# Attention: where the copies of V's last three pieces and of K's second half stand in the order

## The chip, the cores and the metric

The kernel runs on one core of one Trainium2 chip. The metric is the device time of one execution in microseconds (us). A profiled execution also gives a span, from the first instruction to the last, with the instructions of each engine in it: TensorE (PE, with its weight loads as PEld), VectorE (DVE), ScalarE (ACT), GpSimd (POOL) and SyncE (SP).

## The reference

One block of a streaming encoder on x (1 x 512 x 1024, float32) and a memory mem (1 x 256 x 1024): two recurrent branches side by side, merged into x; then attention from x into the memory; then a gated feed-forward layer with a short convolution; a final norm. The change lies in the attention:

```
def cross_attention(h, m, w_q, w_kv, w_o):
    q = (h @ w_q).reshape(bsz, s, X_HEADS, X_HEAD_DIM)          # 4 heads of 256
    kv = m @ w_kv
    k = kv[..., :D_MODEL].reshape(bsz, -1, X_HEADS, X_HEAD_DIM)
    v = kv[..., D_MODEL:].reshape(bsz, -1, X_HEADS, X_HEAD_DIM)
    sc = jnp.einsum('bqhd,bkhd->bhqk', q, k).astype(jnp.float32) * (X_HEAD_DIM ** -0.5)
    pr = jax.nn.softmax(sc, axis=-1).astype(v.dtype)
    o = jnp.einsum('bhqk,bkhd->bqhd', pr, v).reshape(bsz, s, D_MODEL)
    return o @ w_o
```

h is the normed x, m the normed memory.

## The kernel before

**Precision and tiles.** A float32 matrix product is done as three matmuls on a split operand: `hi` is the value rounded to the matmul's format, `lo` the rest. So each operand is first copied (ScalarE writes `hi`) and then subtracted (VectorE writes `lo`); `mm3` (lines 169 to 173) issues hi x hi, hi x lo and lo x hi. Weights come in pieces of 128 x 1024 through `stream` (lines 106 to 127): SyncE loads a piece (four buffers), ScalarE and VectorE split it (three buffers). `dense` (lines 192 to 200) makes one output block of 128 x 512 from one such piece, in 24 matmuls.

**What the stage is given.** K and V are computed from the memory at the start of the kernel and put away in DRAM (`dK`, `dV`), 1024 x 256 values each. The stage before attention is the merge into x (`mix_ps`); behind attention come its output product (`co_ps`) and the feed-forward layer.

**The attention stage** (lines 1057 to 1152). K and V are brought back in eight pieces of 128 x 512 by `load_kv`: four of K (`load_kv("K", 0)` for heads 0 and 1, `load_kv("K", 1)` for heads 2 and 3) and four of V (two rows of memory blocks, each in two halves, of which the first half serves heads 0 and 1). Every piece is loaded into one of five buffers (`KVB = 5`) by a load that ScalarE issues, then copied by ScalarE and subtracted by VectorE into K2 or V2 (lines 1094 and 1095). A piece's buffer comes free with its subtraction; pieces six to eight wait for the buffers of pieces one to three.

`q_head` makes a head's q in two blocks of 24 matmuls (`q_ps`) and splits it (lines 1107 and 1108). `attend` takes a head through: for each of four tiles of 128 queries, 6 matmuls of scores (`sc_ps`, two PSUM buffers), the maximum and a bias on VectorE (lines 1123 and 1124), exp on ScalarE (`ex`, line 1126), division by the sum, and two transposes on TensorE (`prT_ps`); then the split of the transposed probabilities (`prT`, lines 1133 and 1134), and two blocks of 6 matmuls with V (`o_ps`, one PSUM buffer), each split into `o2` (lines 1141 and 1142). The program is written as q of head 0, then for each head its attention and q of the next head; the second half of K is loaded and copied, in the text, behind q of head 1.

**What sets the order.** The text is not the order in which an engine works. A planner takes the instructions with their dependencies and lays out one sequence for each engine by its own estimate of when each could go, with the place in the text as priority, so that q of the next head is put among the scores of this one. On the chip each engine follows its sequence: an instruction that waits holds all that stands behind it on that engine, and a load that ScalarE issues has its place in ScalarE's sequence. `tc.issue_after(ins)` sets, for the planner, that what is written inside it comes behind `ins` on the same engine; it makes no signal. GpSimd in the meantime adds up feed-forward weights in DRAM (`dS`), each step held back to a matmul of this stage (`sum_behind`, lines 177 to 181); SyncE loads the weights ahead.

Of the kernel before, what the change touches and what calls it, by code (L numbers as in the profile page):

```python
# [3 lines left out]

# [54 lines left out]
def hybrid_block_kernel(ctx: ExitStack, tc: tile.TileContext, xT_d, mT_d, pv_d, cst_d, win_d, wk_d, wv_d,  # L59
                        lup_d, gup_d, rga_d, rgx_d, wba_d, wbb_d, wmix_d, wq_d, wo_d, wfi_d, wfo_d, out_d):  # L60
    nc = tc.nc
    V, S, PE = nc.vector, nc.scalar, nc.tensor
# [12 lines left out]
    def mm_ps(name):  # L75
        return pmm.tile([P, T], F32, tag="mm", name=name)

    def rw_ps(name, pool=None, tag="rw", **kw):
        return (pool or prw).tile([P, T], F32, tag=tag, name=name, **kw)
# [89 lines left out]
    def mm3(ps, lh, ll, rh, rl, start, stop, **kw):  # L169
        first = PE.matmul(ps, lh, rh, start=start, stop=False, **kw)  # L170
        PE.matmul(ps, lh, rl, start=False, stop=False, **kw)  # L171
        PE.matmul(ps, ll, rh, start=False, stop=stop, **kw)  # L172
        return first
# [18 lines left out]
    def dense(ps, units, rhs, nkb, nsum=0):  # L192

        for kb in range(nkb):
            wh, wl = units.next()
            rh, rl = rhs(kb)
            ins = mm3(ps, wh, wl, rh, rl, kb == 0, kb == nkb - 1)
            if kb * nsum % nkb < nsum:
                sum_behind(ins)
        return ins  # L200
# [845 lines left out]
    for m in range(KB):  # L1046
        xin = pm.tile([P, T], F32, tag="xin", name=f"xin{m}")
        nc.scalar.dma_start(xin, xT_d[:, m, :])
        ps = mm_ps(f"mix_ps{m}")
# [14 lines left out]
    def probs(hd):  # L1064
        return pk.tile([P, 2, 2, T], F32R, tag="prT", name=f"prT{hd}", bufs=2)
# [14 lines left out]
    V2 = pk.tile([P, 2, 2, D], F32R, name="V2")  # L1080

    def load_kv(what, i):
        for h in range(2):
            kv = pk.tile([P, T], F32, tag="kv", name=f"kv{what}{i}_{h}", bufs=KVB)
            if what == "K":
                ks = slice(4 * i + 2 * h, 4 * i + 2 * h + 2)
                hi, lo = K2[:, 0, ks], K2[:, 1, ks]
                kv = kv.rearrange("p (m n) -> p m n", n=NMEM)
                nc.scalar.dma_start(kv, dK[ks].rearrange("m p n -> p m n"))
            else:  # L1090
                cs = slice(h * T, (h + 1) * T)
                hi, lo = V2[:, 0, i, cs], V2[:, 1, i, cs]
                nc.scalar.dma_start(kv, dV[i, :, cs])
            S.copy(hi, kv)
            V.tensor_tensor(lo, kv, hi.bitcast(F32), ALU.subtract)

    load_kv("K", 0)
    for i in range(2):
        load_kv("V", i)
    uq = Units(wq_d, "wq")  # L1100

    def q_head(hd, nsum=2):
        q2 = pk.tile([P, 2, 2, T], F32R, tag="q2", name=f"q2_{hd}", bufs=2)
        for i in range(2):
            ps = mm_ps(f"q_ps{hd}_{i}")
            dense(ps, uq, lambda kb: (hx[:, 0, kb, :], hx[:, 1, kb, :]), KB, nsum + i * (nsum > 0))
            S.copy(q2[:, 0, i, :], ps)
            V.tensor_tensor(q2[:, 1, i, :], ps, q2[:, 0, i, :].bitcast(F32), ALU.subtract)
        return q2

    def attend(hd, q2):
        prT = probs(hd) if hd else prT0
        prps = [rw_ps(f"prT_ps{hd}_{i}", pat, "prT", bufs=2) for i in range(2)]
        for tt in range(4):
            sl = slice(tt * P, (tt + 1) * P)
            ps = rw_ps(f"sc_ps{hd}_{tt}", pat, "sc", bufs=2)
            for i in range(2):
                kb = 2 * hd + i
                PE.matmul(ps[:, :NMEM], q2[:, 0, i, sl], K2[:, 0, kb, :], start=(i == 0), stop=False)
                PE.matmul(ps[:, :NMEM], q2[:, 0, i, sl], K2[:, 1, kb, :], start=False, stop=False)  # L1120
                PE.matmul(ps[:, :NMEM], q2[:, 1, i, sl], K2[:, 0, kb, :], start=False, stop=(i == 1))
            st = pk.tile([P, 4], F32, tag="smst", name=f"smst{hd}_{tt}", bufs=4)
            V.tensor_reduce(st[:, 0:1], ps[:, :NMEM], AX.X, ALU.max)
            V.tensor_tensor(st[:, 1:2], st[:, 0:1], nrx[:, tt:tt + 1], ALU.mult)
            ex = pk.tile([P, NMEM], F32, tag="ex", name=f"ex{hd}_{tt}", bufs=3)
            S.activation(ex, ps[:, :NMEM], AF.Exp, scale=rxc[:, tt:tt + 1], bias=st[:, 1:2],
                         accum_out=st[:, 2:3])
            V.reciprocal(st[:, 3:4], st[:, 2:3])
            V.tensor_scalar(ex, ex, st[:, 3:4], None, ALU.mult)
            for i in range(2):  # L1130
                PE.transpose(prps[i][:, sl], ex[:, i * P:(i + 1) * P], ident)
        for i in range(2):
            S.copy(prT[:, 0, i, :], prps[i])
            V.tensor_tensor(prT[:, 1, i, :], prps[i], prT[:, 0, i, :].bitcast(F32), ALU.subtract)
        for i in range(2):
            kb = 2 * hd + i
            ps = rw_ps(f"o_ps{kb}", pat, "o")
            for n in range(2):
                cs = slice(kb * P, (kb + 1) * P)
                mm3(ps, V2[:, 0, n, cs], V2[:, 1, n, cs], prT[:, 0, n, :], prT[:, 1, n, :], n == 0, n == 1)  # L1140
            S.copy(o2[:, 0, kb, :], ps)
            V.tensor_tensor(o2[:, 1, kb, :], ps, o2[:, 0, kb, :].bitcast(F32), ALU.subtract)

    q2 = q_head(0, 0)
    for hd in range(4):
        attend(hd, q2)
        if hd < 3:
            q2 = q_head(hd + 1)
        if hd == 0:
            load_kv("K", 1)  # L1150

    pk_ctx.close()

# [25 lines left out]
    for m in order:  # L1179
        ps = mm_ps(f"co_ps{m}")  # L1180
# [4 lines left out]
        i = m % 4  # L1185
# [264 lines left out]
    for k in K4:  # L1450
        ks = slice(k, min(k + 4, HB))
# [11 lines left out]
    for k in K4:  # L1463
        ks = slice(k, min(k + 4, HB))
# [82 lines left out]
```

## Time and profile before

| | us |
|---|---|
| three runs | 885.95, 889.65, 891.37; median 889.65 |
| the profiled execution | 888.2 |
| its span | 886.4 |
| TensorE busy in it | 865.9 |
| VectorE, ScalarE, GpSimd busy | 676.7, 513.6, 132.5 |

The three runs lie within 0.6% of each other. Times in the trace are counted from the start of the span. "L1094" is line 1094 of the kernel before; `kvK<-dK` is an instruction that writes a buffer `kvK` from `dK`, with the numbers of the buffers left out. A busy TensorE is not TensorE at its peak: matmuls overlap, and their ends are modelled, so an idle stretch is read from what the profile lists as idle before an instruction.

### The profile page before, as it was taken

To read this page: it belongs to the slowest core of one execution; us is meant where nothing else is said; L and a number is where in the kernel's file an instruction comes from. 1 tells how busy PE (TensorE), PEld (TensorE's weight loads), DVE (VectorE), ACT (ScalarE), POOL (GpSimd) and SP (SyncE) were. 2 spreads that over 40 slices of the span, in tenths; PEclk is the share of its full clock that TensorE was granted. 3 is DMA by queue.
4 is the path that set the end of the run, shared out by engine and by line. 5 is a ranking of instruction groups with operands and counts; after the bars stand their busy time and mean duration, and the time that the engine had idled before them with its cause. 6 is when DMAs were issued, how large, how long until landed. Compare 5 with 4: busy or idle time off the path is not lost.

```text
span 886.4 us, 15940 instructions
## 1 busy us (share of the span) xinstructions
PE 865.9 (98%) x6197; PEld 755.0 (85%) x6197; DVE 676.7 (76%) x1096; ACT 513.6 (58%) x788; POOL 132.5 (15%) x163
## 2 busy tenths in 40 slices
PE   8999999999999999999989999999999999999996
PEld 7778878888877677888867778999999999999896
DVE  6796598777967777685565568898888788998674
ACT  7575676643337676243454456766665566767563
POOL 0101222021101012001112211112111211111100
PEclk9999999999999999999999999999999999999999
DMA  8878899678997379858877868899999999998963
GB/s 279 301 254 215 209 223 238 191 197 240 260 236 156 74 197 230 229 157 239 220 205 169 203 150 191 239 258 285 300 257 297 262 320 277 249 280 207 293 208 95
DMA packets 97562, 201.37 MB, mean 227 GB/s; under 512 B 19600, under 2 KB 30992, under 8 KB 97424
## 3 DMA queue, kind: packets, MB, share of 16 engines
q1 hardware_dynamic: 62240, 118.57, 40.5%
q0 software_dynamic: 25504, 67.38, 37.3%
q10 hardware_dynamic: 9744, 14.42, 4.9%
q8 instruction: 48, 0.79, 0.4%
q14 instruction: 26, 0.21, 0.1%
HBM read 188.54 MB, written 78.12 MB: 301 GB/s over the span
## 4 chain that ended last, share of the span: by engine, by line
PE 80%; DMA 8%; DVE 7%; ACT 3%; issue 1%; ACTq 0%; SPq 0%; DVEq 0%
PE in_ps L171 7%; PE in_ps L172 7%; PE in_ps L170 7%; PE fx_ps L170 3%; PE fx_ps L172 3%; PE fx_ps L171 3%; PE fyz_ps L170 3%; PE fyz_ps L171 3%; PE fyz_ps L172 3%; DMA wfi_r<-in_wfi 2%; DMA wfo_r<-dOs 2%; PE co_ps L172 2%; PE mix_ps L171 2%; PE co_ps L171 2%; PE mix_ps L170 2%; PE co_ps L170 2%
## 5 line engine op out<-in xcount | busy, mean ns | idle before, releaser
L171 PE MATMUL in_ps<-hT,win_h 128*128 128x512 f32 x304 | 121.0, 398 | 0.4 <-DVE hT L387 0.4
L172 PE MATMUL in_ps<-hT,win_l 128*128 128x512 f32 x304 | 121.3, 399 | 0.0
L170 PE MATMUL in_ps<-hT,win_h 128*128 128x512 f32 x304 | 120.5, 398 | 0.3 <-DVE pr L589 0.3
L136 ACT CAST wfi_h<-wfi_r 128x1024 fp32r<-128x1024 f32 x77 | 80.9, 1051 | 64.4 <-PE fyz_ps L171 17.2
L137 DVE TENSOR_TENSOR wfi_l<-wfi_r,wfi_h 128x1024 fp32r<-128x1024 f32 x77 | 93.9, 1220 | 23.5 <-ACT wfi_h L136 23.4
L485 POOL DMA_DIRECT2D dS<-in_wfi x66 | 66.7, 1034 | 299.2 <-PE in_ps L170 96.4
L171 PEld LDWEIGHTS in_ps<-hT,win_h 128*128 128x128 f32 x304 | 57.1, 188 | 14.6 <-DVE hT L387 1.0
L170 PEld LDWEIGHTS in_ps<-hT,win_h 128*128 128x128 f32 x304 | 57.1, 188 | 13.4 <-DVE pr L589 0.7
L172 PEld LDWEIGHTS in_ps<-hT,win_l 128*128 128x128 f32 x304 | 57.1, 188 | 12.9 <-issue 0.7
L521 POOL DMA_DIRECT2D dOs<-in_wfo x54 | 39.8, 784 | 171.3 <-PE fx_ps L170 46.0
L123 DVE TENSOR_TENSOR win_l<-win_r,win_h 128x1024 fp32r<-128x1024 f32 x38 | 46.3, 1220 | 24.1 <-ACT win_h L122 20.6
L122 ACT CAST win_h<-win_r 128x1024 fp32r<-128x1024 f32 x38 | 39.9, 1050 | 40.0 <-PE in_ps L171 35.6
L1358 DVE TENSOR_TENSOR wfo_l<-wfo_r,wfo_h 128x1024 fp32r<-128x1024 f32 (+1 forms) x39 | 46.9, 1206 | 14.4 <-ACT wfo_h L1357 14.4
L1357 ACT CAST wfo_h<-wfo_r 128x1024 fp32r<-128x1024 f32 (+1 forms) x39 | 40.3, 1035 | 30.3 <-DMA wfo_r<-dOs 14.0
L172 PE MATMUL ox_ps<-go,wfo_l 128*128 128x256 f32 x176 | 48.8, 277 | 1.2 <-DVE wfo_l L1358 1.2
L170 PE MATMUL ox_ps<-go,wfo_h 128*128 128x256 f32 x176 | 48.7, 277 | 0.6 <-ACT wfo_h L1357 0.6
L170 PE MATMUL fx_ps<-hr,wfi_h 128*128 128x256 f32 x176 | 48.7, 277 | 0.3 <-ACT sn L1293 0.3
L170 PE MATMUL fx_ps<-hq,wfi_h 128*128 128x256 f32 x176 | 48.8, 277 | 0.1
L172 PE MATMUL fyz_ps<-hq,wfi_l 128*128 128x256 f32 x176 | 48.7, 277 | 0.0
L172 PE MATMUL fx_ps<-hq,wfi_l 128*128 128x256 f32 x176 | 48.7, 277 | 0.0
L170 PE MATMUL fyz_ps<-hq,wfi_h 128*128 128x256 f32 x176 | 48.7, 277 | 0.0
L171 PE MATMUL fx_ps<-hq,wfi_h 128*128 128x256 f32 x176 | 48.6, 276 | 0.0
(432 smaller groups left out, 2689.7 us busy)
## 6 DMA issues: line engine op xcount, KB each, us to landing
dS<-in_wfi POOLq DMA_DIRECT2D x66, 512.0 KB, 7.6
wfi_r<-dS SPq DMA_DIRECT2D x44, 512.0 KB, 6.9
win_r<-in_win SPq DMA_DIRECT2D x38, 512.0 KB, 5.3
wfi_r<-in_wfi SPq DMA_DIRECT2D x33, 512.0 KB, 5.6
dS<-dS POOLq DMA_DIRECT2D x22, 512.0 KB, 5.7
dOs<-in_wfo POOLq DMA_DIRECT2D x12, 512.0 KB, 7.8
wk_r<-in_wk SPq DMA_DIRECT2D x8, 512.0 KB, 5.8
wv_r<-in_wv SPq DMA_DIRECT2D x8, 512.0 KB, 5.2
```

The source lines that it names most:

```text
L122: casts.append(S.copy(hi[:, o:o + n], raw[:, o:o + n]))
L123: V.tensor_tensor(lo[:, o:o + n], raw[:, o:o + n], hi[:, o:o + n].bitcast(F32), ALU.subtract)
L136: S.copy(hi, raw)
L137: V.tensor_tensor(lo, raw, hi.bitcast(F32), ALU.subtract)
L170: first = PE.matmul(ps, lh, rh, start=start, stop=False, **kw)
L171: PE.matmul(ps, lh, rl, start=False, stop=False, **kw)
L172: PE.matmul(ps, ll, rh, start=False, stop=stop, **kw)
L485: return lambda: nc.gpsimd.dma_start(s(out), src, **kw)
L521: yield lambda k=k, w=w, src=src: nc.gpsimd.dma_start(dO[n, m][:, k * P:(k + w) * P], src, **kw)
L1357: S.copy(hi[:, :n], raw[:, :n])
L1358: V.tensor_tensor(lo[:, :n], raw[:, :n], hi[:, :n].bitcast(F32), ALU.subtract)
```

## The change

`load_kv` now only issues the two loads and returns what is to be split; the new `split_kv` makes the copies and subtractions, and can put the copies, on ScalarE, behind a given instruction. The first half of K and the first piece of V are loaded and split as before. The other three pieces of V are loaded at the same place in the text, but their copies are written behind q of head 0 and ordered behind the copy of q's second block (`last["q"]`). The second half of K is loaded, in the text, ahead of head 0's attention, and its copies are written ahead of q of head 1 and ordered behind the second copy of head 0's transposed probabilities (`last["p"]`). The number of loads, copies, subtractions and matmuls, and the buffers and their order, stay as they were.

```
     def load_kv(what, i):
+        copies = []
         for h in range(2):
             kv = pk.tile([P, T], F32, tag="kv", name=f"kv{what}{i}_{h}", bufs=KVB)
...
                 nc.scalar.dma_start(kv, dV[i, :, cs])
-            S.copy(hi, kv)
+            copies.append((hi, lo, kv))
+        return copies
+
+    def split_kv(copies, behind=None):
+        for hi, lo, kv in copies:
+            with tc.issue_after(behind.ins) if behind is not None else nullcontext():
+                S.copy(hi, kv)
             V.tensor_tensor(lo, kv, hi.bitcast(F32), ALU.subtract)
 
-    load_kv("K", 0)
-    for i in range(2):
-        load_kv("V", i)
+    split_kv(load_kv("K", 0))
+    vs = load_kv("V", 0)
+    split_kv(vs[:1])
+    vs = vs[1:] + load_kv("V", 1)
     uq = Units(wq_d, "wq")
...
-            S.copy(q2[:, 0, i, :], ps)
+            last["q"] = S.copy(q2[:, 0, i, :], ps)
...
-            S.copy(prT[:, 0, i, :], prps[i])
+            last["p"] = S.copy(prT[:, 0, i, :], prps[i])
...
+    last = {}
     q2 = q_head(0, 0)
+    split_kv(vs, last["q"])
+    ks = load_kv("K", 1)
     for hd in range(4):
         attend(hd, q2)
+        if hd == 0:
+            split_kv(ks, last["p"])
         if hd < 3:
             q2 = q_head(hd + 1)
-        if hd == 0:
-            load_kv("K", 1)
```

More of the change, by code (lines that the diff above doesn't have):

```diff
@@ L1 @@
 import math
-from contextlib import ExitStack
+from contextlib import ExitStack, nullcontext
 from itertools import chain, islice
```

## The prediction

> **What bounds the kernel now.** I read the page first, then the busy time by stretch, then the chain of waits inside the attention stage, then the instructions of ScalarE, TensorE and VectorE around the one hole that the stretches show.
>
> ```profile
> span 886.4 us, 15940 instructions
> ...
> PE 865.9 (98%) x6197; PEld 755.0 (85%) x6197; DVE 676.7 (76%) x1096; ACT 513.6 (58%) x788; POOL 132.5 (15%) x163
> ```
>
> TensorE is busy 865.9 of 886.4 us, so everything that any change without touching its matmuls can win in the whole kernel is 20.5 us, and only what is lost in the stage that is edited is in reach here. The next view gives stretches: length, busy time of TensorE (and how many matmuls), its weight loads, VectorE, ScalarE, GpSimd, then the granted clock, the DMA share and GB/s.
>
> ```profile
> 430.00:450.34 20.34, 20.34 (x93) 16.36 (x91) 12.74 (x22) 11.31 (x18) 1.87 (x2) 1.00 0.85 222
> 450.34:458.50 8.16, 4.48 (x26) 3.63 (x25) 3.54 (x10) 2.29 (x7) 1.87 (x2) 1.00 0.78 246
> 458.50:521.00 62.50, 62.50 (x320) 49.43 (x321) 35.78 (x89) 27.30 (x59) 13.05 (x14) 1.00 0.79 175
> 521.00:560.00 39.00, 39.00 (x187) 32.41 (x186) 32.59 (x63) 26.49 (x51) 6.73 (x7) 1.00 0.76 177
> 560.00:800.00 240.00, 239.48 (x2096) 238.23 (x2096) 213.91 (x287) 157.21 (x227) 39.70 (x55) 1.00 0.95 277
> ```
>
> The attention stage lies in the first three rows. TensorE is full in the first and the third; in 450.34 to 458.50 it loses 8.16 - 4.48 = 3.68 us. That is all the stage has to give. The clock is 1.00 throughout, so the hole costs its own length and nothing behind it. The chain of waits says what the hole is:
>
> ```profile
> 445.44 4.27 DMA kvV<-dV
> 449.75 7.43 DMA kvK<-dK
> 457.20 0.62 ACT K L1094
> ```
>
> A load of K's second half, issued at 449.75, lands 7.43 us later; the copy of it (0.62 us) is on the path. ScalarE's own order shows why (ACTq rows are loads that it issues; the bracket is idle time before the row and what ended it):
>
> ```profile
> 444.51 0.62 ACT L1094 CAST V<-kvV 128x512 fp32r<-128x512 f32 x1
> 444.52 1.31 ACTq L1093 DMA_DIRECT2D kvV<-dV  x3
> 446.95 1.05 ACT L122 CAST wq_h<-wq_r 128x1024 fp32r<-128x1024 f32 x1 [1.82 <-PE q_ps L171]
> 448.41 1.95 ACT L1094 CAST V<-kvV 128x512 fp32r<-128x512 f32 x3 [0.41 <-DMA kvV<-dV]
> 449.75 0.90 ACTq L1089 DMA_DIRECT2D kvK<-dK  x2
> 450.27 1.06 ACT L1107 CAST q<-q_ps 128x512 fp32r<-128x512 f32 x2
> 457.20 0.62 ACT L1094 CAST K<-kvK 128x512 fp32r<-128x512 f32 x1 [5.87 <-DMA kvK<-dK]
> 457.73 0.56 ACT L1126 ACTIVATE ex<-sc_ps,smst,rxn 128x256 f32<-128x256 f32 x1
> ...
> 464.36 1.07 ACT L1133 CAST prT<-prT_ps 128x512 fp32r<-128x512 f32 x2 [1.26 <-PE prT_ps L1131]
> 467.18 0.59 ACT L1141 CAST o<-o_ps 128x512 fp32r<-128x512 f32 x1 [1.74 <-PE o_ps L172]
> ```
>
> The first exp of head 0 (457.73) stands behind a copy of K that head 2 alone reads, and that copy sits 5.87 us on its load. On VectorE the bias of that exp (L1124, two of them in 0.28 us) was there long before:
>
> ```profile
> 454.29 0.28 DVE L1124 TENSOR_TENSOR smst<-smst,rxn 128x1 f32<-128x1 f32 x2
> 457.85 0.69 DVE L1095 TENSOR_TENSOR K<-kvK,K 128x512 fp32r<-128x512 f32 x1 [3.29 <-ACT K L1094]
> ...
> 467.80 0.69 DVE L1142 TENSOR_TENSOR o<-o_ps,o 128x512 fp32r<-128x512 f32 x1 [1.53 <-ACT o L1141]
> ```
>
> So the exp was ready at 454.29 + 0.14 = 454.43 and ran at 457.73, 3.30 us late. TensorE's rows show what that did:
>
> ```profile
> 441.49 0.39 PE L170 MATMUL q_ps<-hx,wq_h 128*128 128x512 f32 x1
> ...
> 446.98 0.39 PE L170 MATMUL q_ps<-hx,wq_h 128*128 128x512 f32 x1
> ...
> 450.90 0.39 PE L1119 MATMUL sc_ps<-K,q 128*128 128x256 f32 x1 [0.55 <-ACT q L1107]
> ...
> 458.43 0.38 PE L1119 MATMUL sc_ps<-K,q 128*128 128x256 f32 x1 [3.14 <-ACT ex L1126]
> ...
> 465.00 0.50 PE L170 MATMUL o_ps<-prT,V 128*128 128x512 f32 x1
> ...
> 486.99 0.28 PE L1119 MATMUL sc_ps<-K,q 128*128 128x256 f32 x1
> ```
>
> Two holes, 0.55 + 3.14 = 3.69 us, the 3.68 of the stretch. The second: the third score tile needs one of two PSUM buffers, which the late exp holds. The first: the scores wait for q's copy. A block of 24 q matmuls takes 446.98 - 441.49 = 5.49 us, 0.229 each; head 0's second block ended by 447.2, but its q was copied at 450.27, behind three copies of V.
>
> **K's second half behind the probabilities.** Same two loads, two copies and two subtractions; nothing is added, and an order on one engine needs no new signal. The copies leave their place ahead of the first exp and go behind the prT copies, which end at 464.36 + 1.07 = 465.43. Then the exp goes at 454.43, frees its score buffer at about 455.0, and TensorE, which had q matmuls to 455.1 (458.43 less 3.14, less the overlap of the last one), does not wait: the 3.14 us go whole. Next late would be the second exp, 0.56 us behind the first, as before. At the new place the copies need 2 x 0.62 = 1.24 us of ScalarE, in a gap of 1.74 ahead of the o copy, and 2 x 0.69 = 1.38 us of VectorE in a gap of 1.53: cost 0. Were the gaps gone, at most 1.4 us would come ahead of the o copy, and head 1's q matmuls stand beside it. The reader of these pieces, head 2's scores at 486.99, is 20 us off.
>
> The loads move too: written ahead of head 0's attention, they can be issued right behind V's three, from 444.52 + 1.31 = 445.83, for 0.90 us, before the weight copy at 446.95. What is queued behind them on ScalarE is that copy and q's; the second load also needs the buffer of V's first piece (copied by 444.51 + 0.62 = 445.13, then the 0.69 us subtraction: 445.8), so it adds at most some tenths. Landing 7.43 us after 446.7 they are there by 454.2, 11 us before their copies. They pass GpSimd's sums and SP's load of the next weights, which are wanted tens of microseconds later.
>
> **V's last three pieces behind q.** The q copy of the second half now waits only for its matmuls (447.2) and the weight copy (446.95 + 1.05 = 448.00): done at 448.6, so the scores can begin 2.3 us sooner than at 450.90. That is worth nothing by itself, since TensorE filled this time with head 1's q; it bears only on the 0.55 us. With seven or more q matmuls set ahead of the scores (446.98 + 7 x 0.229 = 448.6) the wait is 0; with none it is 448.6 - 447.2 = 1.4. Before, the order had (450.34 - 446.98) / 0.229, about 15, and still waited 0.55. I take 0.6, next to that row, and keep 0 and 1.4. V itself is first read at 465.00, 14 us after its last copy: covered.
>
> V's copies now stand between q's copy and the first exp, so their loads become the thing to watch. The last was issued at 445.44 and landed at 449.71; copied by 450.4. The exp would be ready 454.43 - 450.90 = 3.5 us behind the first score, at 448.6 + 3.5 = 452.1: 1.7 us of cover, cost 0.
>
> **Sum.** 3.14 + 0.55 - 0.6 = 3.1 us, between 2.3 and 3.7. The profiled execution took 888.2 us (886.4 of span and 1.8 around it), which gives 885.1. The median of the three runs, 889.65, lies 1.45 above it and would give 886.55; I forecast the middle, 885.8.
>
> **The rivals.**
>
> *V takes K's place in part.* If V's last piece lands as K's did, 7.43 us after its issue, at 452.9, and all three copies (1.95) are still to do, the exp goes at 454.8, 2.7 late. The 3.30 before made 3.14 of hole, so this makes 2.6, plus the 0.6: the gain is 0.5. Landings between give 0.5 to 3.1, in the middle 1.8: 888.2 - 1.8 = 886.4. For it: both kinds of load are 256 KB and K's took longer. Against: V's own rows are the nearer ones.
>
> ```profile
> kvK<-dK ACTq DMA_DIRECT2D x4, 256.0 KB, 6.2
> kvV<-dV ACTq DMA_DIRECT2D x4, 256.0 KB, 4.2
> ```
>
> (KB each and median us to landing, of the stage's loads.) By the Trainium skill, DMA: Bandwidth & Descriptors, "Anatomy of one DMA", a transfer takes some 2.0 us and its bytes over 436 GB/s; that is an estimate of 2.6 us for 256 KB, fitted for GpSimd's path. By it V would land at 448.0 and this rival and the next would have no chance; the trace's 4.2 and 6.2 differ from it, and they decide.
>
> *Slower: K's loads beside V's.* The loads of K move from 4 us behind V's to directly beside them, in a stretch where the DMA share is 0.85 already. If that holds V's pieces back, the first exp waits for V longer than it did for K. It turns where the exp is over 3.25 us late (3.1 of hole and the 0.6), at 455.35; less the three copies, from a landing at 453.4, 8.0 us after the issue. One of the longest loads in the chain of waits took this:
>
> ```profile
> 678.05 11.37 DMA wfi_r<-in_wfi
> ```
>
> With 11.37 us (for 512 KB) it is V at 456.8, exp at 458.8, a hole of 6.5 + 0.6, 3.4 us slower, 891.6. Midway, at 9.5 us, the exp goes at 456.9, 4.8 late: 4.6 + 0.6 - 3.7 = 1.5 slower, 889.7. Against it: V's loads still stand first on ScalarE's queue. The Trainium skill, the same page, "Issuing engines are not separate DMA queues", says that loads of all issuing engines interleave on the same 16 DMA engines; by that rule the K loads would slow V's, and the trace agrees as far as 256 KB took 4.27 us in one place and 7.43 in another.
>
> *Given back later.* In 560 to 800 the DMA share is 0.95 and the chain passes through weight loads; were the loads the bound there, an earlier start would only wait longer, and the time stays 888.2. Against: TensorE lost 0.52 us in those 240, and each load waits for a buffer that TensorE's progress frees, so it starts earlier by the same amount.
>
> *Not what it says.* The planner that orders the engines sees other due times, and lays out everything behind this point anew, with a shift of over 1% either way. No row speaks for it.
>
> **How the numbers follow.** The forecast 0.63, V in part 0.14, slower 0.10, given back 0.08, a new layout 0.05. The range: the forecast's own is the highest gain from the lowest run shown (885.95 - 3.7 = 882.2) to the least gain from the median (889.65 - 2.3 = 887.4). Giving back ends at 888.2 to 889.65 and the slower case at 889.7, midway, so the upper end is 890.4; a little below for the layout: 881.8 to 890.4. A measurement tells 1% from no change, 8.9 us; no case but a new layout reaches that, half of it each way: faster 0.03, same 0.94, slower 0.03.
>
> **What would show it.** Right: no K copy among ScalarE's rows between q's copy and the first exp, no idle time of some 6 us on a K load there, q's second copy at about 448.0, scores from 448 to 449, K's copies between the prT and o copies, and in the stretch of head 0 a TensorE that loses 0 to 1.4 us, all of it on q. Wrong in part: the first exp or V's copies idle on V's loads. Wrong: a hole ahead of the third score tile again, o matmuls that wait for a late o copy, or more loss past 560 than the 0.52 us of before.

## The result, and the profile after

Over 22 executions of each, the kernel before took 888.56 us (885.12 to 892.34) and the changed one 886.34 us (881.48 to 891.27). The ratio is 0.9964, with a 95% interval of 0.9949 to 0.9980: 3.2 us less, between 1.8 and 4.5. (The ratio is the record's estimate from these executions, not the quotient of the two medians; those lie 2.2 us apart, which is inside the interval too.) The forecast was 3.1 us less, 885.8 us, no change by the 1% bound. The profiled execution of the changed kernel took 885.64 us, with a span of 883.9, against 888.2 and 886.4.

TensorE in the attention stage of the changed kernel, by stretch (length, busy time and matmuls of TensorE, then of its weight loads, VectorE, ScalarE and GpSimd, the granted clock, the DMA share, GB/s):

```profile
430.00:447.00 17.00, 17.00 (x79) 13.96 (x78) 10.41 (x19) 8.48 (x13) 1.15 (x1) 1.00 0.80 216
447.00:470.00 23.00, 23.00 (x125) 18.72 (x124) 17.20 (x40) 13.64 (x28) 5.15 (x6) 1.00 0.92 241
470.00:521.00 51.00, 51.00 (x251) 39.45 (x250) 26.99 (x62) 21.15 (x43) 10.92 (x12) 1.00 0.73 163
```

The hole is gone altogether, not only its larger part: 23.00 of 23.00 us busy where the two waits had cost 3.68. ScalarE's rows show the new order:

```profile
444.41 0.81 ACTq L1094 DMA_DIRECT2D kvV<-dV  x2
447.00 1.05 ACT L122 CAST wq_h<-wq_r 128x1024 fp32r<-128x1024 f32 x1 [2.00 <-PE q_ps L171]
447.96 1.07 ACT L1115 CAST q<-q_ps 128x512 fp32r<-128x512 f32 x2
448.91 1.15 ACT L1101 CAST V<-kvV 128x512 fp32r<-128x512 f32 x2
449.69 0.38 ACTq L1090 DMA_DIRECT2D kvK<-dK  x1
449.95 0.63 ACT L1101 CAST V<-kvV 128x512 fp32r<-128x512 f32 x1
450.10 0.48 ACTq L1090 DMA_DIRECT2D kvK<-dK  x1
453.08 0.56 ACT L1134 ACTIVATE ex<-sc_ps,smst,rxn 128x256 f32<-128x256 f32 x1 [2.50 <-DVE smst L1132]
...
459.93 1.08 ACT L1141 CAST prT<-prT_ps 128x512 fp32r<-128x512 f32 x2 [1.16 <-PE prT_ps L1139]
460.89 1.15 ACT L1101 CAST K<-kvK 128x512 fp32r<-128x512 f32 x2
462.77 0.59 ACT L1149 CAST o<-o_ps 128x512 fp32r<-128x512 f32 x1 [0.73 <-PE o_ps L172]
```

The first exp now waits only for its own bias (2.50 us, VectorE), no longer for a load; K's copies stand between prT and o, and 0.73 us is left there. But K's two loads are issued at 449.69 and 450.10, as late as before (449.75): moving them forward in the text did not move them on ScalarE, where they stand behind the second and the third of V's late copies. TensorE's rows:

```profile
448.41 0.39 PE L170 MATMUL q_ps<-hx,wq_h 128*128 128x512 f32 x1
448.64 0.34 PE L1127 MATMUL sc_ps<-K,q 128*128 128x256 f32 x1
...
454.19 0.28 PE L1127 MATMUL sc_ps<-K,q 128*128 128x256 f32 x1
...
460.57 0.50 PE L170 MATMUL o_ps<-prT,V 128*128 128x512 f32 x1
```

The scores begin at 448.64, seven q matmuls of head 1 behind head 0's, and nothing in brackets stands at either place where TensorE had waited. VectorE has the least room, 0.35 us ahead of the o subtraction:

```profile
461.76 1.28 DVE L1102 TENSOR_TENSOR K<-kvK,K 128x512 fp32r<-128x512 f32 x2
463.39 0.69 DVE L1150 TENSOR_TENSOR o<-o_ps,o 128x512 fp32r<-128x512 f32 x1 [0.35 <-ACT o L1149]
```

From the first q matmul to the first matmul of the feed-forward stage, by their starts in the traces, the kernel before took 556.48 - 434.98 = 121.5 us and this one 552.87 - 435.04 = 117.8: 3.7 us less. From there to the end it took 331.0 against 329.9, so the span gained only 2.5.

### The profile page after: what moved, and what is told of

It reads as the page before. It is cut to its first block, busy times and chain, and to the rows that moved or that the text cites. A ratio compares the mean times of both kernels' runs of the same rounds, so it can differ in the third digit from the quotient of the medians.

```text
span 883.9 us, 15941 instructions
## 1 busy us (share of the span) xinstructions
PE 867.5 (98%) x6197; PEld 756.8 (86%) x6197; DVE 676.8 (77%) x1096; ACT 513.3 (58%) x788; POOL 132.6 (15%) x163
## 4 chain that ended last, share of the span: by engine, by line
PE 82%; DVE 7%; DMA 6%; ACT 3%; issue 1%; DVEq 0%; SPq 0%; ACTq 0%
PE in_ps L171 7%; PE in_ps L172 7%; PE in_ps L170 7%; PE fx_ps L170 4%; PE fx_ps L172 4%; PE fx_ps L171 4%; PE fyz_ps L170 3%; PE fyz_ps L172 3%; PE fyz_ps L171 3%; DMA wfi_r<-in_wfi 2%; DMA wfo_r<-dOs 2%; PE q_ps L171 2%; PE co_ps L170 2%; PE mix_ps L171 2%; PE q_ps L172 2%; PE co_ps L172 2%
## 5 line engine op out<-in xcount | busy, mean ns | idle before, releaser
L170 PE MATMUL fyz_ps<-hq,wfi_h 128*128 128x256 f32 x176 | 48.8, 278 | 0.3 <-ACT p L1290 0.3
L170 PE MATMUL fx_ps<-hq,wfi_h 128*128 128x256 f32 x176 | 48.9, 278 | 0.2
L171 PE MATMUL fyz_ps<-hq,wfi_h 128*128 128x256 f32 x176 | 48.6, 276 | 0.0
```

## The experiments

The theory: what TensorE waits for in this stage is a ScalarE that stands on a load; what the change wins is the sum of those waits, and everything behind moves along. The rivals: the gain comes from q being copied sooner; V's loads take the place of K's; part of the gain is given back in the feed-forward stage. For the four variants with a ratio, times are against 35 executions of the kernel before on the same chip (median 889.04 us). The microseconds given go by the ratio; the medians of `k_only`, `v_only` and `k_load_first` lie 1.8, 1.0 and 3.7 us below 889.04, that of `before_twice` 2.4 above.

**K's part alone** (`k_only`). Against the changed kernel:

```
-    vs = load_kv("V", 0)
-    split_kv(vs[:1])
-    vs = vs[1:] + load_kv("V", 1)
+    split_kv(load_kv("V", 0))
+    split_kv(load_kv("V", 1))
...
-    split_kv(vs, last["q"])
```

> Only K's part is done: the copies of K's second half stand behind head 0's probabilities, its loads are written ahead of head 0's attention; all four pieces of V are copied ahead of q as before. Theory (the 3.14 us hole is the first exp standing behind the K copy, and closing it is nearly the whole gain): no wait ahead of the third score tile, the wait for q's copy stays at about 0.55 us, TensorE idles 0.5 to 0.8 us in the stage, and the time falls by 2.9 to 3.2 us, ratio about 0.9965. Rival (the gain comes from q being copied, and the scores begun, 2.3 us sooner): a hole stays in the stage and the ratio is 0.999 to 1.001.

Measured: ratio 0.9973 (0.9959 to 0.9987), 2.4 us less, between 1.2 and 3.6. The one wait of TensorE in its stage is the one for q:

```profile
452.30 0.39 PE L1126 MATMUL sc_ps<-K,q 128*128 128x256 f32 x1 [0.46 <-ACT q L1114]
```

Its first exp waits for VectorE, not for K, although K's loads took as long here as in the kernel before (the second line is their time from issue to landing):

```profile
455.92 0.56 ACT L1133 ACTIVATE ex<-sc_ps,smst,rxn 128x256 f32<-128x256 f32 x1 [3.18 <-DVE smst L1131]
DMA to landing us min/median/max: 7.3/7.4/7.4
```

The stage took 118.3 us. So K's part alone closes the 3.1 us hole, and the rival falls: only the wait for q is left, although q is copied as late as before, and its unchanged time (0.999 and more) lies just outside the interval.

**V's part alone** (`v_only`).

```
-    ks = load_kv("K", 1)
...
-        if hd == 0:
-            split_kv(ks, last["p"])
         if hd < 3:
             q2 = q_head(hd + 1)
+        if hd == 0:
+            split_kv(load_kv("K", 1))
```

> Only V's part is done: V's last three copies stand behind q of head 0; K's second half is loaded and copied as before. Theory: the scores begin at about 448.6, but the first exp still stands behind the K copy, whose load is issued at about 449.7 and lands near 457; the exp goes at 457.5, the hole ahead of the third score tile is 3.5 to 4.0 us, so V's part gains nothing alone: ratio 0.999 to 1.001. Rival (the earlier q is what counts): hole under 1.5 us, ratio 0.997 or less.

Measured: ratio 0.9993 (0.9977 to 1.0008). ScalarE stands on K's load again (first row: the load's issue):

```profile
450.78 0.38 ACTq L1090 DMA_DIRECT2D kvK<-dK  x1
...
456.07 0.62 ACT L1101 CAST K<-kvK 128x512 fp32r<-128x512 f32 x1 [4.36 <-DMA kvK<-dK]
456.60 0.56 ACT L1134 ACTIVATE ex<-sc_ps,smst,rxn 128x256 f32<-128x256 f32 x1
```

```profile
457.30 0.39 PE L1127 MATMUL sc_ps<-K,q 128*128 128x256 f32 x1 [1.57 <-ACT ex L1134]
```

The time is where the theory had it, and the rival's 0.997 lies outside the interval. But the hole is 1.57 us, not the 3.5 to 4.0 of the theory, and only just above the 1.5 that the rival set as its upper end. The load took 456.07 - 450.78 = 5.3 us where it had taken 7.4. One trace of each kernel cannot say whether the hole follows the load, so three of the kernels were profiled again.

**The same kernels again** (`before_b`, `before_c`, `v_only_b`, `after_b`; nothing edited).

> The kernel before once more, for one trace. Theory: the hole ahead of the third score tile is as long as the K load lets it be, some 4.3 us less than that load takes from issue to landing (7.43 us gave 3.14); with a landing of 5 to 7.5 us it is 0.7 to 3.2 us. Rival: the hole is fixed by the order of the engines, 3.1 us again whatever the load took.

> As the run ahead of it, a third trace of the kernel before: the hole is the landing less 4.3 us (theory), or 3.1 us (rival).

> V's part alone once more. In the first trace of it the K load took 5.3 us and the hole was 1.57: the landing less 3.7. Theory: the same relation, so a hole between 1 and 3.8 us, always more than in the kernel before for the same landing. Rival: the hole stays at 1.6 us, because the earlier q shortened it.

> The changed kernel once more. Theory: no wait of TensorE in the attention stage again, whatever the loads of K take; from the first matmul of the feed-forward stage to the end the time differs from the first trace by up to 2 us either way, as it does between executions of the kernel before. Rival (part of the gain is given back there): the feed-forward stage is longer than in each trace of before, by about 1 us.

The table has, for these traces and those shown ahead of them, the first K load from issue to the start of its copy, the wait ahead of the third score tile, all waits of TensorE in the stage, and the time in three parts: to the first q matmul, from there to the first feed-forward matmul, and from there to the end of the span (us, from the starts in each trace).

| trace | K load | third tile | all waits | start | stage | rest |
|---|---|---|---|---|---|---|
| before | 7.4 | 3.1 | 3.7 | 435.0 | 121.5 | 329.9 |
| before_b | 6.8 | 2.4 | 3.0 | 435.1 | 122.5 | 330.5 |
| before_c | 6.9 | 2.5 | 3.0 | 434.8 | 121.0 | 330.0 |
| v_only | 5.3 | 1.6 | 1.6 | 436.2 | 119.3 | 331.0 |
| v_only_b | 5.7 | 2.1 | 2.1 | 434.5 | 119.8 | 332.6 |
| k_only | not waited for | 0 | 0.5 | 436.5 | 118.3 | 332.4 |
| after | not waited for | 0 | 0 | 435.0 | 117.8 | 331.0 |
| after_b | not waited for | 0 | 0 | 433.7 | 117.9 | 330.4 |

The hole follows the load: the load less 4.3 or 4.4 us in the three traces of before, less 3.6 or 3.7 in the two with V's part, whose scores begin sooner. The rival of a hole fixed by the order (3.1 each time) falls, and so does that of `v_only_b` (1.6 again; it was 2.1, with a load 0.4 us longer). With V's part alone the wait would be 0.7 us longer for the same load; the load was shorter in both traces. Why is not shown. The stage is 117.9 us plus its waits, within 0.2 us, in all rows but one (before_b, below). So the stage was some 2 us shorter in the two traces of V's part alone, because K's load was; whether V's part makes it so is not shown, and the time (0.6 us less, between 2.0 less and 0.7 more) shows no gain. The rest was 0.9 and 2.4 us longer in them than the mean of before. What V's part adds to K's is the 0.46 us that TensorE still waits for q in `k_only`; the two times, 2.4 and 3.2 us less, cannot be told apart by their intervals. The rest of `k_only` holds a fall of the clock at 826 us (last section).

**K's loads ahead of V's** (`k_load_first`). Against the changed kernel:

```
-    vs = load_kv("V", 0)
-    split_kv(vs[:1])
-    vs = vs[1:] + load_kv("V", 1)
+    vs = load_kv("V", 0, (0,))
+    split_kv(vs)
+    ks = load_kv("K", 1)
+    vs = load_kv("V", 0, (1,)) + load_kv("V", 1)
...
-    ks = load_kv("K", 1)
```

(`load_kv` has the halves to load as a third argument.)

> As the change, but the two loads of K's second half stand ahead of V's last three loads on ScalarE's queue, so that V's pieces are loaded last, at 446 to 448. It measures the cover of V's copies and the slower rival of the prediction. Theory (a load of 256 KB beside K's lands in 4 to 5 us, V's copies end by 453.5, the exp is not held): no hole above 0.5 us, ratio about 0.996. Rival (with K's loads beside them V's take 7 us and more): V's last copy ends at 456 to 457, the exp goes at 457 to 458, a hole of 2 to 3 us, ratio 0.999.

Measured: ratio 0.9962 (0.9939 to 0.9985), 3.4 us less, and no wait of TensorE in the stage, which took 117.6 us. ScalarE's rows:

```profile
443.10 0.89 ACTq L1090 DMA_DIRECT2D kvK<-dK  x2
444.09 0.42 ACTq L1094 DMA_DIRECT2D kvV<-dV  x1
445.78 1.05 ACT L122 CAST wq_h<-wq_r 128x1024 fp32r<-128x1024 f32 x1 [2.07 <-PE q_ps L171]
445.84 0.82 ACTq L1094 DMA_DIRECT2D kvV<-dV  x2
446.73 1.07 ACT L1116 CAST q<-q_ps 128x512 fp32r<-128x512 f32 x2
448.42 1.40 ACT L1101 CAST V<-kvV 128x512 fp32r<-128x512 f32 x2 [0.62 <-DMA kvV<-dV]
451.18 0.62 ACT L1101 CAST V<-kvV 128x512 fp32r<-128x512 f32 x1 [1.36 <-DMA kvV<-dV]
452.66 1.05 ACT L122 CAST wq_h<-wq_r 128x1024 fp32r<-128x1024 f32 x1 [0.86 <-PE q_ps L171]
453.62 0.56 ACT L1135 ACTIVATE ex<-sc_ps,smst,rxn 128x256 f32<-128x256 f32 x1
```

Here ScalarE does wait for V, 0.62 and 1.36 us, and still no matmul does: V's last copy ends at 451.8, ahead of the weight copy and the exp. And the loads of V, beside and behind K's, took from issue to landing (least, median, most):

```profile
DMA to landing us min/median/max: 3.3/4.3/4.9
```

The slower rival, which needed 8.0 us, has no ground even with K's loads put in front.

**The wait doubled** (`before_twice`). Against the kernel before; each of the last two K pieces is loaded twice:

```
-                nc.scalar.dma_start(kv, dK[ks].rearrange("m p n -> p m n"))
+                for _ in range(1 + i):
+                    nc.scalar.dma_start(kv, dK[ks].rearrange("m p n -> p m n"))
```

> The kernel before, with each of the two loads of K's second half done twice in a row into the same buffer, the second waiting for the first: the same wait, doubled. It asks whether time lost in this stage reaches the end. Theory (everything behind moves along with TensorE): TensorE's idle time in the stage grows from 3.7 to between 8 and 13 us, and the time grows by the difference, 4 to 9 us, all of it. Rival (the feed-forward stage's loads use the lost time to run ahead, and give part of it back): the time grows by half of the added idle time or less.

Measured: ratio 1.0042 (1.0020 to 1.0064), 3.7 us more, between 1.8 and 5.7. The waits did not come as expected, 4.2 us in all and not 8 to 13: besides the 0.46 for q,

```profile
457.75 0.39 PE L1120 MATMUL sc_ps<-K,q 128*128 128x256 f32 x1 [1.10 <-ACT ex L1127]
...
466.49 0.50 PE L170 MATMUL o_ps<-prT,V 128*128 128x512 f32 x1 [2.67 <-ACT prT L1134]
```

ScalarE's rows show what held it:

```profile
456.09 1.05 ACT L122 CAST wq_h<-wq_r 128x1024 fp32r<-128x1024 f32 x1 [4.55 <-DMA kvK<-dK]
...
465.33 0.62 ACT L1095 CAST K<-kvK 128x512 fp32r<-128x512 f32 x1 [3.40 <-DMA kvK<-dK]
465.86 1.07 ACT L1134 CAST prT<-prT_ps 128x512 fp32r<-128x512 f32 x2
```

It first stood until the first load had landed and the repeated one could be issued. The planner put the first two exps ahead of the K copy, so the first hole shrank, and a second came up where the probabilities' copy stood behind the other K copy. The stage took 124.0 us, 2.3 more than the mean of the three traces of before (121.7), although the waits grew by 0.5 to 1.2 only. The rest is in the clock (same columns as the first table of stretches):

```profile
463.00:465.00 2.00, 0.81 (x5) 0.34 (x3) 0.00 (x0) 0.00 (x0) 0.72 (x1) 1.00 1.09 224
465.00:467.00 2.00, 0.51 (x2) 0.47 (x3) 1.02 (x2) 1.59 (x3) 0.00 (x0) 1.00 1.06 226
467.00:469.00 2.00, 2.00 (x6) 1.32 (x6) 1.54 (x3) 1.53 (x2) 0.00 (x0) 0.64 0.51 191
469.00:471.00 2.00, 2.00 (x10) 1.87 (x9) 1.24 (x3) 0.59 (x1) 0.00 (x0) 0.51 0.28 49
```

Behind the 2.67 us hole the granted clock fell to half for 3.4 us. As a test of what reaches the end, the run speaks against the rival: the stage added 2.3 us and the time 3.7 (2.4 by the medians), with a lower end of 1.8, above the half of the stage's 2.3 that would be left if the rest gave half of it back. It was weaker than planned, since the added time was small and the stage is known from one trace.

## Why the prediction was right, point by point

- **The hole and its cause.** Right. One K copy on its load held the first exp; with only that part done (`k_only`) the third score tile waits for nothing, and the time falls by 2.4 us (1.2 to 3.6), against 3.2 (1.8 to 4.5) for the whole change.
- **The term for q's copy, 0.6 us left over.** Mis-sized. The planner set exactly seven q matmuls of head 1 ahead of the scores, the number that the prediction gave as the point of no wait, and the wait is 0 in both traces. The stage gained 3.7 us in the first pair of traces, not 3.1.
- **V's copies ahead of the first exp, cost 0.** Right, with more room than the 1.7 us worked out: ScalarE idled 2.50 us before that exp.
- **K's copies between prT and o, cost 0.** Right: 0.73 us is left on ScalarE, 0.35 on VectorE.
- **K's loads issued early.** Wrong, without effect. They stayed among V's copies, at 449.69. A place earlier in the text was not an order on the engine; only `k_load_first`, where the text puts them ahead of V's loads, moved them, and it gained nothing measurable over the change (0.9962 against 0.9964).
- **The clock, a hole costs its own length.** Wrong as a rule, though it held in the trace that it was read from. In `before_b` the same hole, shorter, was followed by a clock of half (next section but one), 1.6 us on top. So the hole cost more than its length in some executions of the kernel before, which the sum does not have.
- **Given back later.** Open. The stage gained 3.8 us by the means of its traces (121.7 to 117.9), the time 3.2, between 1.8 and 4.5. From the first feed-forward matmul to the end it took 329.9 to 330.5 us in the three traces of before, 331.0 and 330.4 in the two of the change, and 328.5 to 332.6 in the other variants. A loss of half a microsecond there is neither shown nor excluded.
- **The slower rival.** V's loads landed in 3.2 to 4.8 us in the changed kernel, and in 3.3 to 4.9 with K's loads in front. It did not come up.

## What to carry to other kernels

An engine that works in a fixed order stops on the first load that is late, whatever stands behind it: look for a copy whose reader is far off and which stands ahead of something that is wanted now, and put it behind that, where the engine idles anyway. The cost of such a stop here was the time from the load's issue to its landing, less 4.3 us: TensorE had work for 5.5 us behind the issue (449.75 to 455.29 in the first trace), and 1.2 us went from the landing to the held score (457.20 to 458.43). The 4.3 changes when the order is laid out anew (3.6 or 3.7 with V's part). An order that matters has to be looked up on the engine: every copy that moved here had an order set on ScalarE (whether the text alone would have moved it was not tried), while the loads, which had none, stayed where they were when written ahead of the attention and moved only when written ahead of V's.

## What the runs showed of the hardware that was not expected

The granted clock can fall behind a hole that is shorter than one behind which it did not fall. In `before_b`, which runs the kernel before:

```profile
455.00:458.00 3.00, 0.59 (x4) 0.17 (x2) 0.61 (x2) 1.26 (x4) 1.17 (x1) 1.00 0.68 164
458.00:460.00 2.00, 2.00 (x11) 1.77 (x12) 1.62 (x4) 2.00 (x5) 0.00 (x0) 0.83 0.81 140
460.00:462.00 2.00, 2.00 (x9) 1.89 (x8) 1.29 (x7) 1.05 (x3) 0.00 (x0) 0.50 0.98 141
462.00:464.00 2.00, 2.00 (x9) 1.51 (x9) 1.97 (x7) 0.66 (x2) 0.19 (x1) 0.82 0.55 225
464.00:466.00 2.00, 2.00 (x12) 1.50 (x10) 0.02 (x1) 0.51 (x2) 0.95 (x1) 1.00 0.28 16
```

Here the wait was 2.41 us (455.55 to 457.96), and the clock was half from 459.3 on, for 3.4 us; the stage took 122.5 us, which is 117.9, the 3.0 of waits, and 1.6 more. Behind 3.14 us in the first trace of before, and behind 2.5 in the third, it stayed at 1.00; behind 2.67 in `before_twice` it fell. So a hole of 2.4 to 3.1 us in this stage cost the clock in two of four traces, and those of 2.1 and less in none.

The length of the hole is not what decides. In each of the ten traces all recorded changes of the clock lie whole multiples of 3.413 us apart. Cut into stretches of that length, with the ends on those changes, the four traces give (columns as above; the time that TensorE was idle is the length less its busy time):

```profile
453.71:457.12 3.41, 1.58 (x7) 0.95 (x6) 0.85 (x4) 0.00 (x0) 1.17 (x1) 1.00 0.62 231
457.12:460.53 3.41, 2.10 (x15) 1.97 (x16) 2.31 (x5) 3.33 (x8) 0.00 (x0) 1.00 1.03 148
...
452.95:456.36 3.41, 2.13 (x12) 1.48 (x10) 0.95 (x4) 0.00 (x0) 1.17 (x1) 1.00 0.88 315
...
455.90:459.31 3.41, 1.35 (x10) 1.30 (x11) 1.55 (x4) 2.57 (x7) 0.91 (x1) 1.00 0.65 110
459.31:462.72 3.41, 3.41 (x13) 2.82 (x12) 2.71 (x10) 1.74 (x6) 0.00 (x0) 0.50 1.00 204
...
464.15:467.56 3.41, 1.07 (x4) 0.72 (x5) 1.58 (x3) 1.90 (x4) 0.00 (x0) 1.00 1.04 236
467.56:470.98 3.42, 3.42 (x13) 2.93 (x13) 2.20 (x4) 1.81 (x3) 0.00 (x0) 0.50 0.30 83
```

(in turn `before`, `before_c`, `before_b`, `before_twice`). The 3.14 and the 2.5 us are cut by an end, so that no stretch has more than 1.83 and 1.28 us idle; `before_b` has 2.06 in one and `before_twice` 2.34, and the next stretch runs at half clock, which costs half its length, 1.7 us. Over all ten traces, from the first rise of the clock to the end of the kernel, it fell behind every such stretch with 1.9 us idle or more and behind none with 1.6 or less; between the two, 1.64 to 1.83, both occurred (in `k_only` it fell at 826 us behind 1.64, in short waits). Since ends of matmuls are modelled, the limit is not known more closely.

The Trainium skill, TensorE: Matmul & The Clock Gate, "HAM oscillation", gives about 3.4 us of idle time as the bound for such a fall; by its Part 1 the window in which activity is counted runs freely, so that the place of a hole in it matters. That the outcome differs between executions of one kernel agrees with the second; the falls behind 2.41 and 2.67 us are below the first, and here the measurement decides.

The first 256 KB load of K's second half, at nearly the same place in the order, took 6.7 to 7.4 us to land in the three traces of before and 7.3 in `k_only`; it took 5.3 and 5.7 with V's part alone, 5.0 and 6.2 in the two of the change, but also 5.7 in `before_twice`, which has V's copies where they were. V's loads, a few microseconds earlier, took 3.6 to 5.0 in the traces of before and of V's part alone. In each of these traces SyncE issued a 512 KB load of weights (`wo_r`) 0.3 to 0.5 us ahead of K's first, and GpSimd's sums in DRAM ran beside them; which of them makes the difference was not separated.
